# The decode's logits by one VectorE instruction each, in place of a product and a separate sum

## The chip, the cores and the metric

The program runs on one core of a Trainium2 chip. A core has a matrix engine (TensorE, PE in the profile), three engines for element-wise work (VectorE or DVE, ScalarE or ACT, GpSimd or POOL) and queues that start transfers (SP's and POOL's here). Each engine takes its instructions in order, and engines wait for each other by semaphores. The metric is device time in microseconds (us) for one execution of the whole program, the median of several.

## What is computed

One inference step of one layer of a hybrid decoder, for a prompt of 512 rows (with 16 learned rows ahead of it) and for 8 sequences that decode 4 rows each. All is fp32.

```python
h = rmsnorm(x, g_pre)
q, k, v, ga, cb, cc, ch, gc, ma, mc = jnp.split(h @ w_in, split_offsets(), axis=-1)
a = attend(q, k, v, b_sb).reshape(bsz, t, D_ATTN) * jax.nn.silu(ga)
u = cc * ch
u_ext = jnp.concatenate([conv_hist.astype(u.dtype), u], axis=1)
c = cb * causal_conv(u_ext, w_conv, b_conv) * jax.nn.silu(gc)
merged = (jax.nn.sigmoid(ma + b_gate[:D_MODEL]) * (a @ w_pa)
          + jax.nn.sigmoid(mc + b_gate[D_MODEL:]) * (c @ w_pc))
y = x + rmsnorm(merged @ w_out, g_post)
```

The width is 2048, and `w_in` has 12288 columns. Attention has 8 heads of 128 channels. It is a stick-breaking attention: from logits `z` come weights `sigmoid(z_ts) * prod(1 - sigmoid(z_tj))` over the later keys j, so all logits of a row must be there before its weights. The decode part reads a past of 512 keys for each of its 8 sequences, in 4 pages of 128 rows, found through a page table. Its logits are

```python
z = jnp.einsum('bqhd,bkhd->bhqk', q, k) * (HEAD_DIM ** -0.5) + b_sb[None, :, None, None]
```

that is, for every sequence, page, head and query row, 128 dot products of 128 channels: 8 x 4 x 8 x 4 = 1024 columns of 128 values.

## The kernel before

The kernel is written for a framework that takes a program in order, tracks which tile every instruction reads and writes, sets all semaphores, and orders each engine's instructions by a planner: among the instructions that a timing model says are ready, the one that stands first in the program goes first. `tc.keep_in_program_order` (also bound to the name `pin`) ties instructions together in the order in which they were written.

**TensorE's work.** Most products are made at fp32 accuracy out of three products of split numbers. `w_split` (L233) takes a block of 1024 x 128 weights, rounds it into `whi` on ScalarE (L236) and puts the rest into `wlo` on VectorE (L237). Both tiles have three buffers (pool `whl`). The matmuls of a block follow (L252 in the heads, L887 in the gates), 24 for each range of columns. `seven` (L890) makes a 2 x 2 block product out of seven products instead of eight; for that it forms sums of weight blocks on VectorE (L899, L902, L910, L915), and differences of results (L913, L918). The sums of the activations that it needs (tiles `t_hi`, `t_lo`) are made once, at L853 to L870, ahead of the gates.

**The stages.** After the norm and the first query projections come the attention heads 0 to 3 (`head_now`, L628) and the projections of heads 4 to 7 (`head_later`, L644). Then come the gates of the attention, the convolution (`conv_pair`, L952) and the gates of the merge (loop at L1029 and after), and then the remaining heads, the projections `w_pc`, `w_pa` and `w_out`, and the last norm.

**The decode's logits.** They run beside these stages, as a generator `decode_steps` (L669), of which `dec_step` takes one step at a time at fixed points of the program. There are 16 units (a half of the heads, a sequence) of 4 pages, 64 steps in all. The first 6 units (24 pages, `DEC1`) lie among the heads: `dec_step(64, "part")` at L833 sees that they are done in the program before the activations' sums. The other 10 units (40 pages) lie among the gates: `dec_group` (L813) takes two pages and one page by turns for the first 4 groups, one for the next 16, and again two and one by turns up to group 31. The two parts have pools of their own (`dec1`), whose room is given to later tiles. After them come the weights of the attention and the products with the values.

A step works like this. The query rows of the unit were loaded as two tiles `qt` (`qb` in the profile) of 2 query rows x 4 heads x 128 channels, copied to all 128 partitions. A page's keys `kt` (`kpage`), 128 rows x 512 channels for 4 heads, are loaded over POOL's queue; there are three such buffers. For each of the two query tiles, VectorE makes one product `pr` of 128 x 1024 values (L689). The sums over each 128 channels then go to `z_all`: ScalarE makes them one by one, as a copy into a tile `junk` with an accumulated sum (L695), or VectorE makes 4 or 8 of them at once (L698). The split by hand is: all 8 sums of the first tile on ScalarE; of the second, all 8 on VectorE, but in the second part 4 on ScalarE in each odd page.

## Time and profile before

| | us |
|---|---|
| runs of before | 1638.24, 1635.78, 1639.5 |
| median | 1638.24 |
| the profiled execution | 1638.43 |
| its span, first to last instruction | 1636.8 |
| TensorE (PE) busy | 1596.0 |
| VectorE (DVE) busy | 1259.1 |
| ScalarE (ACT) busy | 969.5 |

The profile names an instruction by its line in the kernel (L689), its engine, its operation and its tiles, output first. "Busy" counts an engine's instructions together without counting overlaps twice. A waiting row reads: engine and line, what released it, then the microseconds in total, the number of times and the longest. A window row has the stretch, its length, busy time and number of instructions for each engine, the clock granted to TensorE (1.00 is full speed), the share of DMA time and GB/s. In a row of a group of instructions stand the number of them, busy time, the mean duration of one in ns, and the engine's idle time before them.

### The profile page before, as it was taken

Reading aid. Unit: us, or ns where it says so; the run is one execution under the profiler, and the core shown is the slowest. Engines: PE = TensorE matmul, PEld = TensorE weight load, DVE = VectorE, ACT = ScalarE, POOL = GpSimd, SP = SyncE. Lnnn points to the kernel's source line nnn. Section 1 sums busy time; section 2 is a strip of 40 time slices with the busy share of each in tenths; the row PEclk is TensorE's granted clock in tenths of the full one; section 3 lists DMA queues with packets and bytes.
Section 4 is the critical chain, followed back from the end, with each engine's and each line's share of the span. In section 5 each row is a group of like instructions: output and inputs, shape, how many; then the busy total and the mean of one; then the engine's idle time right before and its main releaser. Section 6 shows DMA issues by size and latency. Waiting matters only on the chain.

```text
span 1636.8 us, 31603 instructions
## 1 busy us (share of the span) xinstructions
PE 1596.0 (98%) x12172; PEld 1534.2 (94%) x12172; DVE 1259.1 (77%) x1730; ACT 969.5 (59%) x2528; POOL 232.2 (14%) x418
## 2 busy tenths in 40 slices
PE   7999999999999999999999999999999999999997
PEld 6999999999999999999999999989877799999997
DVE  4537887797988988888988888876565567887776
ACT  6237887755775656565676667686544453355562
POOL 0033233322101000100011011002122110000000
PEclk7999999999999999999999999999999999999999
DMA  9254554545554444343555554446888545533345
GB/s 228 77 171 143 157 163 138 152 121 171 157 155 136 130 130 130 116 141 114 148 150 151 156 175 147 128 130 202 263 265 246 179 141 165 183 89 101 106 124 192
DMA packets 306813, 252.72 MB, mean 154 GB/s; under 512 B 11522, under 2 KB 276806, under 8 KB 305846
## 3 DMA queue, kind: packets, MB, share of 16 engines
q1 hardware_dynamic: 278165, 160.45, 34.3%
q0 software_dynamic: 28368, 89.98, 16.9%
q8 instruction: 95, 1.56, 0.4%
q14 instruction: 57, 0.46, 0.1%
q10 hardware_dynamic: 128, 0.27, 0.1%
HBM read 217.95 MB, written 32.71 MB: 153 GB/s over the span
## 4 chain that ended last, share of the span: by engine, by line
PE 75%; ACT 6%; DMA 5%; DVE 4%; issue 3%; POOL 0%; DVEq 0%; SPq 0%; POOLq 0%; ACTq 0%
PE mm L887 24%; PE mm L252 24%; PE o L887 20%; ACT junk L695 3%; PE tp L784 2%; ACT whi L236 2%; PE z L614 1%; DMA raw<-in_w_in 1%; PE o L624 1%; DVE pr L689 1%; DMA gt<-gate_scr 1%; DVE wlo L237 1%; PE z L545 1%; PE z L1319 1%; DMA kpage<-in_cache_k 1%
## 5 line engine op out<-in xcount | busy, mean ns | idle before, releaser
L236 ACT CAST whi<-raw 128x1024 fp32r<-128x1024 f32 x247 | 258.9, 1049 | 253.6 <-PE o L887 75.6
L237 DVE TENSOR_TENSOR wlo<-raw,whi 128x1024 fp32r<-128x1024 f32 x247 | 301.5, 1221 | 56.7 <-ACT whi L236 45.4
L887 PE MATMUL mm<-h_hi,whi 128*128 128x272 f32 (+1 forms) x1152 | 333.8, 290 | 2.8 <-ACT whi L236 2.8
L887 PE MATMUL mm<-h_lo,whi 128*128 128x272 f32 (+1 forms) x1152 | 332.4, 289 | 0.0
L887 PE MATMUL mm<-h_hi,wlo 128*128 128x272 f32 (+1 forms) x1152 | 331.6, 290 | 0.0
L887 PE MATMUL o<-t_hi,whi 128*128 128x272 f32 (+1 forms) x864 | 253.1, 293 | 8.7 <-ACT o L901 5.0
L887 PE MATMUL o<-t_hi,wlo 128*128 128x272 f32 (+1 forms) x864 | 250.8, 290 | 1.3 <-DVE wlo L237 1.3
L887 PE MATMUL o<-t_lo,whi 128*128 128x272 f32 (+1 forms) x864 | 250.6, 290 | 0.0
L237 DVE TENSOR_TENSOR wlo<-s,whi 128x1024 fp32r<-128x1024 f32 x126 | 154.2, 1224 | 100.5 <-ACT whi L236 100.2
L887 PEld LDWEIGHTS mm<-h_hi,whi 128*128 128x128 f32 x1152 | 217.7, 189 | 5.4 <-ACT whi L236 3.7
L887 PEld LDWEIGHTS mm<-h_hi,wlo 128*128 128x128 f32 x1152 | 216.6, 189 | 0.6 <-DVE dr L412 0.4
L887 PEld LDWEIGHTS mm<-h_lo,whi 128*128 128x128 f32 x1152 | 217.1, 188 | 0.1
L695 ACT ACTIVATE junk<-pr 128x128 f32<-128x128 f32 x592 | 182.6, 309 | 28.5 <-DVE pr L689 16.3
L236 ACT CAST whi<-s 128x1024 fp32r<-128x1024 f32 x126 | 131.5, 1044 | 96.9 <-PE o L887 30.8
L252 PE MATMUL mm<-h_hi,whi 128*128 128x280 f32 (+1 forms) x640 | 188.1, 294 | 0.0
L252 PE MATMUL mm<-h_hi,wlo 128*128 128x280 f32 (+1 forms) x640 | 188.0, 295 | 0.0
L252 PE MATMUL mm<-h_lo,whi 128*128 128x280 f32 (+1 forms) x640 | 187.6, 293 | 0.0
L887 PEld LDWEIGHTS o<-t_hi,whi 128*128 128x128 f32 x864 | 163.6, 189 | 15.5 <-ACT o L901 6.1
L887 PEld LDWEIGHTS o<-t_hi,wlo 128*128 128x128 f32 x864 | 163.8, 190 | 2.2 <-DVE wlo L237 2.2
L887 PEld LDWEIGHTS o<-t_lo,whi 128*128 128x128 f32 x864 | 164.4, 190 | 0.0
L689 DVE TENSOR_TENSOR pr<-kpage,qb 128x1024 f32<-128x1024 f32 x128 | 152.3, 1218 | 10.7 <-DMA qb<-q_scr 6.5
L252 PEld LDWEIGHTS mm<-h_hi,whi 128*128 128x128 f32 x640 | 121.4, 190 | 0.7
(392 smaller groups left out, 3402.3 us busy)
## 6 DMA issues: line engine op xcount, KB each, us to landing
raw<-in_w_in SPq DMA_DIRECT2D x192, 512.0 KB, 4.3
kpage<-in_cache_k POOLq DMA_DIRECT2D x64, 256.0 KB, 3.4
qb<-q_scr POOLq DMA_DIRECT2D x32, 512.0 KB, 5.7
vpage<-in_cache_v POOLq DMA_DIRECT2D x64, 256.0 KB, 6.1
raw<-in_w_out SPq DMA_DIRECT2D x32, 512.0 KB, 4.0
gate_scr<-g POOLq DMA_DIRECT2D x32, 272.0 KB, 3.5
gt<-gate_scr POOLq DMA_DIRECT2D x16, 544.0 KB, 4.2
raw<-in_w_pc SPq DMA_DIRECT2D x16, 512.0 KB, 5.9
```

What stands on the lines that cost most here:

```text
L236: act.copy(hi, x)
L237: dve.tensor_sub(lo, x, hi.bitcast(F32))
L252: pe.matmul(o, lhsT=w, rhs=r[:, t0:t1], start=(k == 0 and n == 0), stop=(k == nk - 1 and n == 2))
L545: pe.matmul(zt[:m, c0:c0 + n], lhsT=l[:, s0:s0 + m], rhs=r[:, ts:ts + n], start=(c0 == 0 and i == 0), stop=(i == 2), skip_group_check=True)
L614: pe.matmul(o, lhsT=l, rhs=x, start=False, stop=(i == len(ops) - 1), skip_group_check=True)
L624: pe.matmul(ot[:, ts - NMETA:ts - NMETA + n], lhsT=l[:m, st, :], rhs=x[:m, c0:c0 + n], start=False, stop=(g == GROUPS[-1] and i == 2), ski ...
L689: dve.tensor_mul(pr, kt.unsqueeze(1).broadcast_to([P, 2, 512]), qt))
L695: act.activation(junk, pr[:, t, h * P:(h + 1) * P], AF.Copy, accum_out=z_all[:, pg, b, 4 * hf + h, 2 * i + t:2 * i + t + 1])
L784: pe.matmul(po[32 * j:32 * (j + 1), :], lhsT=lhs, rhs=rhs, start=(pg == 0), stop=(pg == NPG), tile_position=(0, 32 * j), skip_group_check= ...
L887: pe.matmul(o, lhsT=l[:, k, :], rhs=r, start=(start and k == 0 and m == 0), stop=(stop and k == 7 and m == 2), skip_group_check=True)
L1319: pin(pe.matmul(o, lhsT=(m1, m2)[h][:, k + 8 * (q == 1), ts], rhs=two[h][q == 2][:, :, k, :], start=(n == 0), stop=(n == 47)))
```

## The change

The product, the sums on ScalarE and the sums on VectorE go, and with them the tile `pr`. In their place VectorE runs one instruction for each query row and head, which multiplies 128 x 128 keys by the query and sums the products along the channels into one column of `z_all`. Its product goes to a tile `junk` of 128 x 128, now with two buffers. The instructions are not held in program order.

```diff
                         for i, qt in enumerate(qts):
-                            pr = d1.tile([P, 2, 512], F32, name="pr", bufs=2)
-                            tc.keep_in_program_order(
-                                dve.tensor_mul(pr, kt.unsqueeze(1).broadcast_to([P, 2, 512]), qt))
-                            n = 2 if i == 0 else int(said == "logits" and pg % 2)
-                            if n:
-                                for t in range(n):
-                                    for h in range(4):
-                                        junk = d1.tile([P, P], F32, name="junk", bufs=1)
-                                        act.activation(junk, pr[:, t, h * P:(h + 1) * P], AF.Copy,
-                                                       accum_out=z_all[:, pg, b, 4 * hf + h, 2 * i + t:2 * i + t + 1])
-                            if n < 2:
-                                dve.reduce_sum(
-                                    z_all[:, pg, b, 4 * hf:4 * hf + 4, 2 + n:4].rearrange("p h t -> p t h"),
-                                    pr[:, n:].rearrange("p t (h d) -> p t h d", d=P), axis=mybir.AxisListType.X)
+                            for t in range(2):
+                                for h in range(4):
+                                    junk = d1.tile([P, P], F32, name="junk", bufs=2)
+                                    dve.tensor_tensor_reduce(
+                                        out=junk, in0=kt[:, h * P:(h + 1) * P], in1=qt[:, t, h * P:(h + 1) * P],
+                                        scale=1.0, scalar=0.0, op0=ALU.mult, op1=ALU.add,
+                                        accum_out=z_all[:, pg, b, 4 * hf + h, 2 * i + t:2 * i + t + 1])
                         yield
```

## The prediction

> **What bounds the kernel now.** I read the page first: the span, the busy shares, and the chain that ended last.

> ```profile
> span 1636.8 us, 31603 instructions
> PE 1596.0 (98%) x12172; PEld 1534.2 (94%) x12172; DVE 1259.1 (77%) x1730; ACT 969.5 (59%) x2528; POOL 232.2 (14%) x418
> ...
> DVE  4537887797988988888988888876565567887776
> ...
> PE 75%; ACT 6%; DMA 5%; DVE 4%; issue 3%; POOL 0%; DVEq 0%; SPq 0%; POOLq 0%; ACTq 0%
> ```

> TensorE (PE) sets the time: it is busy for 98% of the span and carries 75% of the chain. An average hides the stages, though, and VectorE (DVE) stands at 8 or 9 tenths in most slices of the first two thirds. That is where the decode's logits run, by the first and last start in this row of the tile `junk`:

> ```profile
> L695 ACT ACTIVATION_READ_ACCUMULATOR junk<-pr x592: 185/187/203, 116.8 to 1077.6; 128x1 f32 x198
> ```

> So I cut that stretch into stages and read the windows: stage A (the attention heads), a change-over, stage B (gates and convolution), stage C (gates with more decode pages). The columns are window, PE, PEld, DVE, ACT and POOL busy, clock, DMA share, GB/s. The second fence is the same windows for DVE's instructions on the tile `pr` alone, that is the products and the sums on DVE.

> ```profile
> 115.00:345.00 230.00, 227.77 (x1730) 222.13 (x1729) 188.15 (x258) 174.67 (x597) 72.59 (x130) 0.99 0.51 153
> 345.00:415.00 70.00, 68.65 (x541) 67.84 (x540) 58.62 (x78) 38.88 (x80) 16.80 (x28) 1.00 0.49 152
> 415.00:820.00 405.00, 402.83 (x3177) 401.28 (x3176) 359.93 (x428) 247.63 (x674) 34.72 (x61) 1.00 0.46 136
> 820.00:1080.00 260.00, 254.43 (x1986) 252.16 (x1985) 217.77 (x214) 183.21 (x536) 25.10 (x44) 0.99 0.51 150
> sum 965.00, PE 953.69 PEld 943.41 DVE 824.48 ACT 644.38 POOL 149.22; mean PE 238.42 PEld 235.85 DVE 206.12 ACT 161.10 POOL 37.30
> ```

> ```profile
> 115.00:345.00 230.00, 86.88 (x72) 0.99 0.51 153
> 345.00:415.00 70.00, 4.80 (x4) 1.00 0.49 152
> 415.00:820.00 405.00, 67.98 (x62) 1.00 0.46 136
> 820.00:1080.00 260.00, 59.70 (x54) 0.99 0.51 150
> sum 965.00, DVE 219.36; mean DVE 54.84
> ```

> Three things are to be seen. PE idles 965 − 953.69 = 11.3 us in the whole stretch, which is all that any relief there could win. DVE has 965 − 824.48 = 140.5 us left, 42, 11, 45 and 42 us by stage. ScalarE (ACT) has 320 us left, so it is DVE that must not get more work here. What PE waits for in this stretch:

> ```profile
> PE o L887 <- DVE c L913: 3.5, 4, 1.9
> PE tp L445 <- ACT nat L443: 2.2, 1, 2.2
> PE mm L887 <- ACT whi L236: 2.2, 3, 0.7
> PE o L887 <- ACT o L901: 1.9, 4, 1.4
> PE o L887 <- DVE wlo L237: 1.3, 4, 0.3
> PE o L887 <- ACT s L908: 0.2, 1, 0.2
> ```

> ACT is named for 2.2 + 2.2 + 1.9 + 0.2 = 6.5 us, DVE for 4.8 us.

> **What the change removes.** It takes off DVE the 219.4 us of the fence above (128 products and 64 sums), and off ACT these two rows:

> ```profile
> L695 ACT ACTIVATE junk<-pr 128x128 f32<-128x128 f32 x592 | 182.6, 309 | 28.5 <-DVE pr L689 16.3
> ...
> L695 ACT ACTIVATION_READ_ACCUMULATOR junk<-pr 128x1 f32 x592 | 110.8, 187 | 0.0
> ```

> On ACT that is at most 293 us. Since PE waits only 6.5 us for ACT, the relief is worth 6.5 us at the very most, and I count it as nothing: PE and DVE hide it.

> **What it adds.** Per page, 2 query tiles × 2 rows × 4 heads = 16 instructions on DVE; 64 pages make 1024. The trace of before has no such instruction, so its price is bounded by neighbours. On DVE an instruction's duration overlaps the next one's, so I take start to start:

> ```profile
> 440.31 1.22 DVE L910 TENSOR_TENSOR raw<-raw 128x1024 f32<-128x1024 f32 x1
> 441.45 0.43 DVE L913 TENSOR_TENSOR c<-o,s 128x272 f32<-128x272 f32 x1
> 441.81 1.23 DVE L237 TENSOR_TENSOR wlo<-raw,whi 128x1024 fp32r<-128x1024 f32 x1
> ```

> 1024 elements take 1.14 us and 272 take 0.36 us: 0.78/752 = 1.04 ns an element. So 128 elements take 0.36 − 144 × 1.04 ns = 0.21 us. That is the lower end: the sum comes free. How a sum leaves an engine is seen on ACT:

> ```profile
> 166.31 0.31 ACT L695 ACTIVATE junk<-pr 128x128 f32<-128x128 f32 x1 [0.96 <-DVE pr L689]
> 166.52 0.19 ACT L695 ACTIVATION_READ_ACCUMULATOR junk<-pr 128x1 f32 x1
> 166.74 0.31 ACT L695 ACTIVATE junk<-pr 128x128 f32<-128x128 f32 x1
> ```

> A second instruction reads the accumulator, 0.22 us start to start behind 0.21 us of main work. If DVE's read cost as much as ACT's, a sum would take 0.43 us. But DVE's own tiny instructions are cheaper:

> ```profile
> 592.30 0.16 DVE L970 TENSOR_TENSOR u<-c,cv 128x2 f32<-128x2 f32 x1
> 592.38 0.40 DVE L971 TENSOR_TENSOR u<-c,cv 128x240 f32<-128x240 f32 x1
> ```

> Two elements take 0.08 us. A read on DVE is nearer to this row than to ACT's, so I take 0.21 + 0.09 = **0.30 us** a sum, 4.8 us a page, and keep 0.21 and 0.43 as ends. The highest thinkable value, half rate with the dear read, adds another 128 × 1.04 ns = 0.13 us: 0.56 us.

> [...]

> So DVE loses 219.4 us and gains 1024 × 0.30 = 307.2 us, net +87.8 us. The total would still fit in 140.5 us of idle time, but not all idle time can be filled, because weight splits arrive in bursts. These windows show how full DVE gets now:

> ```profile
> 600.00:640.00 40.00, 39.66 (x316) 39.41 (x315) 37.67 (x46) 24.44 (x66) 4.54 (x8) 1.00 0.50 146
> 680.00:720.00 40.00, 39.67 (x316) 39.39 (x315) 37.37 (x50) 24.86 (x70) 4.65 (x8) 1.00 0.45 133
> 760.00:800.00 40.00, 39.67 (x314) 39.39 (x314) 38.86 (x55) 24.68 (x69) 4.63 (x8) 1.00 0.41 121
> ```

> At 37.4 to 38.9 of 40 us PE begins to lose (0.33 us each). I take the lowest, 37.37/40 = 0.93, as the share that DVE can hold over a stage, and 0.97 as the upper end. A stage then lasts the longer of its present time and DVE's work divided by 0.93. The pages per stage are the products of the `pr` rows by two: 24, 1.5, 20.5, 18.

> - A: 188.15 − 86.88 + 24 × 4.8 = 216.5; /0.93 = 232.8, against 230: +2.8 us.
> - Change-over: 58.62 − 4.80 + 1.5 × 4.8 = 61.0; /0.93 = 65.6, under 70: nothing; DVE's and PE's own work hide it. That cover is thin: if A's pages run late, the sums for the next stage start late.
> - B: 359.93 − 67.98 + 20.5 × 4.8 = 390.4; /0.93 = 419.7, against 405: +14.7 us.
> - C: 217.77 − 59.70 + 18 × 4.8 = 244.5; /0.93 = 262.9, against 260: +2.9 us.

> Together +20.4 us. The thin cover is this row:

> ```profile
> 333.60 0.73 DVE L859 TENSOR_TENSOR r<-h_hi 128x548 f32<-128x548 f32 x1 [0.51 <-ACT junk L695]
> ```

> The block sums of the gate stage start only when the first decode part has freed its room, and ACT's last sum frees it now. That wait of 0.51 us goes; what is late next is DVE's own last sum.

> **Waits and queues.** The edit drops the pinned order of the product and the exchange of `pr` between DVE and ACT; no wait is added, but 16 instructions of one page stand in DVE's in-order queue without a gap: 4.8 us, two pages 9.6 us. Behind them stand the weight splits (L237), and PE waits for those. A split buffer holds three half-blocks, so PE can live on some of them; I put this into the 0.93. On POOL a page's load waits until DVE is done with an earlier page:

> ```profile
> POOL kpage L667 <- DVE pr L689: 305.3, 45, 17.0
> ```

> POOL's other stores queue behind that wait. It is as long as DVE is late, and the same loads are issued, no DMA more. I price it at nothing since POOL is at 14%; without that cover a late load would show as DVE waiting for `kpage`.

> **Rivals.** *Dear sum.* DVE's read costs as ACT's, 0.43 us, 6.88 us a page. By the same steps A is 101.27 + 165.1 = 266.4 (/0.93 = 286.4, +56), change-over 64.1 (/0.93 = 69, nothing), B 433.0 (465.6, +61), C 281.9 (303.1, +43): +160 us, 1798 us. With the cheap read and half rate it is 0.21 + 0.13 + 0.08 = 0.42 us and about the same; with both, 0.56 us, A +110, change-over +2, B +106, C +83: +301 us, 1940 us. For it: ACT's row. Against half rate:

> ```profile
> 9.24 1.28 DVE L205 SCALAR_TENSOR_TENSOR hn<-xt,rs,g_bc 128x1024 f32<-128x1024 f32 x1
> ```

> This two-source fp32 form takes 1.28 us for 1024 elements, where half rate would need 2 × 1024 × 1.04 ns = 2.13 us. [...]

> *It fits.* The planner orders the small, unpinned instructions into the gaps, DVE holds 0.97: A 223, B 402.4, C 252, none longer than now. Time unchanged, 1638 us. For it: 140.5 us of idle time against 87.8 us. Against it: the three full windows, where PE loses already.

> *Faster.* The sum comes free at 0.21 us, 3.36 us a page. DVE's work falls to 181.9, 360.8 and 218.6 us, level or below today's, and PE gets back what it waits for ACT, up to 6.5 us: 1632 us. This decides below about 0.214 us a sum, where 1024 × it equals 219.4 us. Against it: ACT's second instruction.

> *The change doesn't do what it says.* Were the instruction built out of two full passes on DVE, the sum would be 0.42 us, priced above.

> **How the numbers follow.** The profiled execution took 1638.43 us with a span of 1636.8; the median of the runs shown is 1638.24, so I add to 1638.4. Forecast (0.26 to 0.36 us a sum, some tens of us): 1638.4 + 20.4 = **1658.8 us**, chance 0.47. Dear sum 0.25, it fits 0.16, faster 0.12. The range runs from 1632 (the whole relief of ACT) up to 1790, just short of the dear-read sum; beyond it remain the dearest cases. Of "it fits" a little ends outside the bound of 0.2%, about what a measurement of this kernel can tell from no change: faster 0.12, same 0.15, slower 0.73.

> **What would show it.** 1024 instructions on L689's place, each with a read beside it; start to start 0.30 us (0.21 or 0.43 would speak for a rival). DVE near 1347 us of busy time, ACT near 680 to 730. PE's waits for `wlo`, under 2 us in the stretch now, grow to tens of us, most in stage B. A wrong price moves the time by about 1 us per ns once DVE is full; a better order than 0.93 would make the time stay.

## The result and the profile after

The kernel became faster, where slower was forecast.

| | before | after |
|---|---|---|
| median of the runs, us | 1637.23 (1635.78 to 1639.5, 4 runs) | 1621.05 (1620.66 to 1621.63, 4 runs) |
| ratio after/before | | 0.9895, 95% interval 0.9877 to 0.9913 |
| the profiled execution, us (its span) | 1638.43 (1636.8) | 1621.34 (1619.7) |
| forecast, us (range) | | 1658.8 (1632 to 1790) |

The page of after: the span, busy time, VectorE's row of the 40 slices, the chain of waits, and the group of the new instruction (count | busy, mean ns | idle time before them).

```profile
span 1619.7 us, 32340 instructions
PE 1589.6 (98%) x12172; PEld 1531.2 (95%) x12172; DVE 1267.9 (78%) x3586; ACT 755.7 (47%) x1339; POOL 241.0 (15%) x418
...
DVE  4529999666999999999999976676555568887776
...
PE 85%; DMA 4%; issue 2%; DVE 1%; ACT 1%; POOL 1%; DVEq 0%; POOLq 0%; ACTq 0%; SPq 0%
...
L690 DVE CUSTOM_DVE_ANT_0 junk<-kpage,qb 128x128 f32<-128x128 f32 x1024 | 244.7, 286 | 10.6 <-DMA qb<-q_scr 7.0
```

VectorE's busy time rose by 8.8 us and not by the 87.8 forecast, and ScalarE's fell by 213.8. VectorE stands at 9 tenths or more over most of the logits' stretch, fuller than before, and yet TensorE's share of the chain rose from 75% to 85%. The price of a sum stands in the timeline of after (start, duration, instruction):

The read of the accumulator is there, 0.08 to 0.09 us long, but the next instruction starts at the same instant as the read. From sum to sum it is 0.21 us. All 1024 come to 1024 x 0.21 = 215 us, level with the 219.4 us removed.

Where the time came from is seen in the stages A, change-over, B and C in the windows of after, and in one more window behind them, of before (first row) and of after (second):

```profile
115.00:345.00 230.00, 227.21 (x1725) 221.31 (x1724) 205.91 (x986) 114.23 (x223) 79.91 (x130) 0.99 0.50 154
345.00:415.00 70.00, 69.52 (x547) 68.65 (x546) 37.38 (x68) 29.47 (x50) 16.35 (x27) 1.00 0.48 146
415.00:820.00 405.00, 404.88 (x3203) 404.44 (x3202) 390.60 (x1297) 175.29 (x265) 42.28 (x73) 1.00 0.50 148
820.00:1080.00 260.00, 260.00 (x2062) 259.39 (x2061) 211.80 (x499) 129.69 (x183) 21.78 (x37) 1.00 0.47 143
```

```profile
1080.00:1180.00 100.00, 96.26 (x707) 86.49 (x706) 62.93 (x73) 62.50 (x87) 21.08 (x36) 1.00 0.66 204
```

```profile
1080.00:1180.00 100.00, 100.00 (x744) 91.10 (x743) 62.60 (x81) 54.88 (x79) 20.32 (x36) 1.00 0.73 227
```

Read the matmul counts, not the busy time. Over B and C TensorE's busy time grew by only 404.88 + 260.00 − 402.83 − 254.43 = 7.6 us, but it started 3203 + 2062 − 3177 − 1986 = 102 matmuls more. In a row they start every 0.125 to 0.126 us, so it was 12.9 us further on at 1080. Behind that, from 1080 to 1180 us, 3.7 us of idle time went, most of it one wait of 3.1 us for ScalarE's `o`; why it goes was not taken apart. Together that is 16.6 of the 17.1 us by which the profiled times differ; A and the change-over, with one matmul more between them, give nothing.

Why is the progress, 12.9 us, larger than the fall of the idle time, 7.6? One place in before shows both reasons. Its timeline on VectorE, on TensorE, and its windows (the clock is the third number from the end):

```profile
851.08 2.35 DVE L689 TENSOR_TENSOR pr<-kpage,qb 128x1024 f32<-128x1024 f32 x2
853.34 1.22 DVE L910 TENSOR_TENSOR raw<-raw 128x1024 f32<-128x1024 f32 x1
854.48 0.44 DVE L913 TENSOR_TENSOR c<-o,s 128x272 f32<-128x272 f32 x1
```

```profile
852.75 0.29 PE L887 MATMUL mm<-h_lo,whi 128*128 128x272 f32 x1
854.97 0.39 PE L887 MATMUL o<-t_hi,whi 128*128 128x272 f32 x1 [1.93 <-DVE c L913]
```

```profile
853.00:855.00 2.00, 0.07 (x2) 0.03 (x1) 2.00 (x4) 1.91 (x9) 0.54 (x1) 1.00 0.68 193
855.00:858.00 3.00, 3.00 (x14) 3.00 (x15) 3.00 (x3) 1.88 (x8) 0.00 (x0) 0.54 0.26 85
```

Two decode products stand in VectorE's queue ahead of the difference `c` that frees TensorE's result. TensorE waits 1.93 us, and then runs 3 us at a clock of 0.54, with 14 matmuls where 24 would fit (3/0.125). That costs another 1.2 us, which no idle time shows. This is the smaller reason: it is the only such stretch of before in B and C.

The larger one is how idle time is counted. A matmul is recorded with 0.29 us, but the next can start 0.126 us after it, so the idle time leaves out about 0.16 us of every gap. Here the starts are 852.75 and 854.97: 2.22 us in place of 0.126, so 2.09 us are lost where the wait says 1.93. Outside the slow stretch, B and C of before have 43 gaps of more than 0.2 us from start to start. They lose 12.9 us, of which the idle time shows 7.7; in after it is 16 gaps and 1.7 us, of which it shows 0.1. That leaves 3.6 us unseen, and the slow stretch 1.5, of the 5.3 us between progress and idle time.

### The profile page after: what moved, and what is told of

It reads as the page before. It is cut to its first block, busy times and chain, and to the rows that moved or that the text cites. A ratio compares the mean times of both kernels' runs of the same rounds, so it can differ in the third digit from the quotient of the medians.

```text
span 1619.7 us, 32340 instructions
## 1 busy us (share of the span) xinstructions
PE 1589.6 (98%) x12172; PEld 1531.2 (95%) x12172; DVE 1267.9 (78%) x3586; ACT 755.7 (47%) x1339; POOL 241.0 (15%) x418
## 4 chain that ended last, share of the span: by engine, by line
PE 85%; DMA 4%; issue 2%; DVE 1%; ACT 1%; POOL 1%; DVEq 0%; POOLq 0%; ACTq 0%; SPq 0%
PE mm L880 31%; PE o L880 23%; PE mm L252 22%; PE tp L777 2%; PE z L614 1%; PE o L624 1%; DMA gt<-gate_scr 1%; PE z L545 1%; PE z L1312 1%; DMA kpage<-in_cache_k 1%; DMA cr<-c_scr 0%; PE z L1166 0%; DMA gate_scr<-gt 0%; PE tp L442 0%; DMA out<-nat 0%
## 5 line engine op out<-in xcount | busy, mean ns | idle before, releaser
L236 ACT CAST whi<-raw 128x1024 fp32r<-128x1024 f32 x247 | 259.6, 1051 | 327.8 <-PE mm L880 112.5
L237 DVE TENSOR_TENSOR wlo<-raw,whi 128x1024 fp32r<-128x1024 f32 x247 | 301.8, 1222 | 72.4 <-ACT whi L236 60.9
L690 DVE CUSTOM_DVE_ANT_0 junk<-kpage,qb 128x128 f32<-128x128 f32 x1024 | 244.7, 286 | 10.6 <-DMA qb<-q_scr 7.0
L880 PEld LDWEIGHTS mm<-h_lo,whi 128*128 128x128 f32 x1152 | 216.8, 188 | 0.0
L237 DVE TENSOR_TENSOR wlo<-s,whi 128x1024 fp32r<-128x1024 f32 x126 | 154.7, 1228 | 69.5 <-ACT whi L236 68.3
L236 ACT CAST whi<-s 128x1024 fp32r<-128x1024 f32 x126 | 132.0, 1048 | 158.9 <-PE mm L880 50.1
L252 PEld LDWEIGHTS mm<-h_lo,whi 128*128 128x128 f32 x640 | 121.0, 189 | 0.6
```

The costliest lines, as they stand in the source:

```text
L236: act.copy(hi, x)
L237: dve.tensor_sub(lo, x, hi.bitcast(F32))
L252: pe.matmul(o, lhsT=w, rhs=r[:, t0:t1], start=(k == 0 and n == 0), stop=(k == nk - 1 and n == 2))
L690: dve.tensor_tensor_reduce(out=junk, in0=kt[:, h * P:(h + 1) * P], in1=qt[:, t, h * P:(h + 1) * P], scale=1.0, scalar=0.0, op0=ALU.mult, o ...
L880: pe.matmul(o, lhsT=l[:, k, :], rhs=r, start=(start and k == 0 and m == 0), stop=(stop and k == 7 and m == 2), skip_group_check=True)
```

## The experiments

E1 to E8 ask for the relief of ScalarE, the order, and VectorE's load; the others, but for E11, for the size and the rows of the decode's work in VectorE's queue. Each ratio is to the kernel before. "Pinned" is held in program order. "Last sum" is the start of the last logit instruction.

### E1: after, with every sum pinned

```diff
-                                    dve.tensor_tensor_reduce(
+                                    pin(dve.tensor_tensor_reduce(
```

> The changed kernel with each of its 1024 sums held behind the VectorE instruction written before it, so that a page's sums can no longer run ahead of their place in the program. Work on every engine is as in the changed kernel (1621 us). Theory order (the gain comes from the freedom of the sums to fill VectorE's gaps ahead of their place): most of the gain goes, 1631 to 1640 us, and the last sum starts near 1040 to 1080 us instead of 933. Theory relief (the gain comes from the 237 us taken off ScalarE): stays within 1618 to 1625 us.

1622.56 us, ratio 0.9913 (0.9893 to 0.9933). The free sums of after ran ahead (last one at 933 us); pinned, the last starts at 1060, not far from before (last product at 1071, last sum at 1078), and the gain stays. The dropped pin is not its cause.

### E2: before, with the product unpinned

```diff
-                            tc.keep_in_program_order(
-                                dve.tensor_mul(pr, kt.unsqueeze(1).broadcast_to([P, 2, 512]), qt))
+                            dve.tensor_mul(pr, kt.unsqueeze(1).broadcast_to([P, 2, 512]), qt)
```

> The kernel before (1637 us) with the product no longer held in program order; ScalarE keeps its 592 sums. Theory order: 1619 to 1628 us, the last product well before 1000 us. Theory relief: 1634 to 1640 us.

1674.35 us, 1.0232 (1.021 to 1.0255). The products ran ahead (last at 714 us) and ScalarE's sums with them (last at 722), ahead of the roundings `whi` in its queue. TensorE's waits, 115 to 1080 us:

```profile
PE o L886 <- ACT whi L236: 14.1, 10, 2.6
PE mm L886 <- ACT whi L236: 6.5, 12, 1.3
```

The same freedom that costs nothing with the new sums costs 37 us with products and sums on two engines.

### E3: after, with 592 sums on ScalarE over the keys

```diff
+                            n = 2 if i == 0 else int(said == "logits" and pg % 2)
+                            for t in range(n):
+                                for h in range(4):
+                                    aj = d1.tile([P, P], F32, name="aj", bufs=1)
+                                    az = d1.tile([P, 1], F32, name="az", bufs=2)
+                                    act.activation(aj, kt[:, h * P:(h + 1) * P], AF.Copy, accum_out=az)
```

> The changed kernel with 592 sums of 128 channels put back on ScalarE as extra work (over the keys alone, results unused), so ScalarE's load is about that of before. Theory relief: 1632 to 1640 us, with PE waiting for ScalarE again. Theory order: within 1619 to 1626 us.

1648.0 us, 1.0066 (1.0047 to 1.0086). This looked like proof that ScalarE's load costs 27 us, but the page of this kernel names another reason:

```profile
L699 ACT ACTIVATE aj<-kpage 128x128 f32<-128x128 f32 x592 | 182.8, 309 | 79.4 <-DMA kpage<-in_cache_k 68.2
```

ScalarE's in-order queue stood still for 68.2 us at these sums, waiting for transfers of keys. So the run adds a wait and not only load; E11 adds load alone.

### E4: after, with 8 more sums a page

```diff
+                                    if i == 1:
+                                        more = d1.tile([P, 1], F32, name="more", bufs=2)
+                                        dve.tensor_tensor_reduce(
+                                            out=junk, in0=kt[:, h * P:(h + 1) * P], in1=qt[:, t, h * P:(h + 1) * P],
+                                            scale=1.0, scalar=0.0, op0=ALU.mult, op1=ALU.add, accum_out=more)
```

> The changed kernel with the 8 sums of the second query tile made twice in each page: 512 more, about 0.21 us each, 108 us more on VectorE, results unused. This is about the load that the prediction gave VectorE with its price of 0.30 us (88 us more). By the prediction's step (VectorE holds 0.93 of a stage) VectorE's 830 us between 115 and 1062 become 938, which need 1009 us: 1675 to 1690 us. At 0.97: about 1642 us. If gaps can be filled to the end: 1621 to 1630 us.

1653.36 us, 1.0095 (1.0075 to 1.0115), with VectorE's busy time at 1374.1, above the 1347 that the forecast foresaw. It is close to the forecast's time, but not by its reason: the stages B and C lose nothing. The time goes at the change-over (first matmul of the gates' products with `t_hi` at 399.5 us in place of 388.5) and behind the logits, whose last sum now starts at 1152, so that the later products of the decode follow late (the last matmul on `c_hl` ends at 1362.7 in place of 1327.7).

### E5: E1 with 592 sums on ScalarE over what VectorE's sums leave

```diff
-                                    junk = d1.tile([P, P], F32, name="junk", bufs=2)
+                                    junk = d1.tile([P, P], F32, name="junk", bufs=16)
...
+                                    if t < (2 if i == 0 else int(said == "logits" and pg % 2)):
+                                        aj = d1.tile([P, P], F32, name="aj", bufs=1)
+                                        az = d1.tile([P, 1], F32, name="az", bufs=2)
+                                        act.activation(aj, junk, AF.Copy, accum_out=az)
```

> The changed kernel with its sums held in program order (1622.6 us) and, as extra work, ScalarE's 592 sums where the kernel before has them, each over the product tile that a held VectorE instruction left (results unused). Unlike the free sums of the run before this one with ScalarE's load (1648 us), these can't bunch ahead. Theory relief (ScalarE's queue is what PE waited for): 1634 to 1641 us. Theory granularity (PE waited because VectorE worked in pieces of 1.1 to 2.3 us, and ScalarE's load only hurts when it bunches): 1620 to 1626 us.

1664.33 us, 1.0164 (1.0133 to 1.0195). It looked as if the hand-over from VectorE to ScalarE cost 42 us. The edit has a second part, though, 16 result tiles in place of 2; E13 and E14 take the two apart.

### E6: before without ScalarE's sums

```diff
-                            if n:
-                                for t in range(n):
-                                    for h in range(4):
-                                        junk = d1.tile([P, P], F32, name="junk", bufs=1)
-                                        act.activation(junk, pr[:, t, h * P:(h + 1) * P], AF.Copy,
-                                                       accum_out=z_all[:, pg, b, 4 * hf + h, 2 * i + t:2 * i + t + 1])
```

> The kernel before with ScalarE's 592 sums left out (those logits keep zeros); VectorE's products and sums as before. Theory relief: 1619 to 1625 us, the whole gain without any change on VectorE. Theory granularity: 1632 to 1638 us.

The kernel leaves these logits out (they keep zeros, written once by GpSimd). 1632.71 us, 0.9968 (0.9955 to 0.9981): the whole relief of ScalarE alone is worth some 5 us (1637.23 x 0.0032), within the 6.5 that the prediction gave as its most. TensorE still waits 4.3 us for `c`, behind the products.

### E7: before with all sums on VectorE

```diff
-                            n = 2 if i == 0 else int(said == "logits" and pg % 2)
+                            n = 0
...
-                                    z_all[:, pg, b, 4 * hf:4 * hf + 4, 2 + n:4].rearrange("p h t -> p t h"),
+                                    z_all[:, pg, b, 4 * hf:4 * hf + 4, 2 * i:2 * i + 2].rearrange("p h t -> p t h"),
```

> The kernel before with all sums made by VectorE's reduction, 8 at once: ScalarE is relieved of all 592, VectorE gets 84 half-size reductions more or about 71 us (128 reductions of 1.13 us instead of 44 of 1.13 and 20 of 0.59). It tells what the relief is worth when it is paid with a dearer sum. By the run with 108 us more on VectorE (+32 us over 1621) 71 us cost about 21 us: 1640 to 1646 us. If VectorE's gaps take them for nothing: 1620 to 1626 us.

1683.65 us, 1.0275 (1.0244 to 1.0305), at a VectorE busy time of 1332.4, less than E4's 1374.1. It is slower by 46 us where E6, which only drops these sums, is faster by 5: moving them to VectorE does not win by itself, and the form in which VectorE takes them matters. 19.0 us of it are one wait of TensorE at the change-over.

### E8: E1 with 8 more pinned sums a page

The edit is that of E4, with the added sums pinned.

> The changed kernel held in program order (1622.6 us) with the 8 sums of the second query tile made twice, held too: 108 us more on VectorE, which can't be put off. If the 32 us of the free version came from VectorE being full (PE waits for the weight splits): 1650 to 1660 us again or more. If they came from the logits ending late, at 1152 us, and pushing the decode's tail behind: 1630 to 1645 us, with the last sum near 1070 to 1090 us.

1664.49 us, 1.016 (1.013 to 1.0189). TensorE's waits, the start of the block sums of the activations (L859 before, shifted to L857 here), and the windows of B and C:

```profile
PE mm L885 <- ACT whi L236: 20.3, 1, 20.3
```

```profile
L857 DVE TENSOR_TENSOR r<-h_hi x4: 721/722/729, 367.9 to 369.8; 128x548 f32<-128x548 f32 x4
```

```profile
415.00:820.00 405.00, 405.00 (x3206) 404.79 (x3206) 385.41 (x1229) 178.16 (x271) 31.13 (x56) 1.00 0.44 131
820.00:1080.00 260.00, 260.00 (x2067) 260.00 (x2066) 245.48 (x852) 122.61 (x170) 27.09 (x47) 1.00 0.52 159
```

One wait of 20.3 us at the change-over; B and C run as in after, with VectorE at 95 and 94%. The rest is lost behind the logits, whose last sum starts at 1200 us.

### E9 and E10: E1 in one or two larger pieces a query tile

These leave the logits out (the sums don't follow the heads), and keep VectorE's time: one sum over 1536 products in place of eight over 128 (E9), or two over 768 (E10).

```diff
+                            junk = d1.tile([P, 3, 512], F32, name="junk", bufs=1)
+                            pin(dve.tensor_tensor_reduce(
+                                out=junk, in0=kt.unsqueeze(1).broadcast_to([P, 3, 512]),
+                                in1=qt[:, 0, :].unsqueeze(1).broadcast_to([P, 3, 512]),
...
+                                junk = d1.tile([P, 2, 384], F32, name="junk", bufs=2)
+                                pin(dve.tensor_tensor_reduce(
+                                    out=junk, in0=kt[:, 0:384].unsqueeze(1).broadcast_to([P, 2, 384]),
+                                    in1=qt[:, :, 0:384],
```

> The changed kernel held in program order (1622.6 us), but for each query tile one instruction over 3 x 512 channels in place of 8 over 128: VectorE's time for a page stays (2 x 1.67 us against 16 x 0.21 us), in pieces of 1.67 us. It leaves the logits out (the columns get other sums or zeros). ScalarE has no sums, as in the changed kernel. Theory granularity (short urgent instructions of VectorE stand behind long pieces in its queue): 1630 to 1636 us, as the kernel before without ScalarE's sums (1632.7). Theory totals (only the engines' loads count): 1620 to 1625 us.

> As the run before it, in two instructions over 768 channels for each query tile, pieces of 0.87 us (4 a page, 3.5 us). It leaves the logits out too. Granularity: between, 1625 to 1631 us. Totals: 1620 to 1625 us.

E9 1636.2 us, 0.9991 (0.9976 to 1.0005); E10 1650.03, 1.0074 (1.0049 to 1.0099), with VectorE busy for 1263.2 and 1273.6 us. The gain of the change is gone, at nearly the same load and without any sum on ScalarE. But the smaller pieces lose more, which "the size of a piece" does not explain. In the written order of VectorE's instructions, E9's pieces stand alone 116 times out of 128 (it has one result tile); E10's stand in twos 77 times out of 157 rows (it has two). This gave the next theory: the length of the row.

### E11: E1 with 592 sums on ScalarE over constants

```diff
+                                        pin(act.activation(aj, ident, AF.Copy, accum_out=az))
```

> The changed kernel held in program order with 592 sums on ScalarE over a constant tile, held at the places of the sums before, so that they wait neither for VectorE nor for a transfer. If ScalarE's load alone delays PE: 1640 to 1665 us, as with the sums over VectorE's products (1664). If those 42 us came from ScalarE waiting in its queue for VectorE's products: 1623 to 1630 us.

1620.67 us, 0.9896 (0.9871 to 0.9922), with ScalarE busy for 965.9 us, as much as before. ScalarE's load as such costs nothing that the time shows (E1, without it, has 1622.56).

### E12 and E13: E1 with 8 and with 16 result tiles

Nothing but the number of result tiles changes. How many sums the planner writes in a row depends on it: with 2 tiles mostly two, with 16 mostly 8 to 16.

```diff
-                                    junk = d1.tile([P, P], F32, name="junk", bufs=2)
+                                    junk = d1.tile([P, P], F32, name="junk", bufs=16)
```

> The kernel after with every sum held in program order, as in the first experiment, and with 8 result tiles (junk) instead of 2. Nothing else differs: the same 1024 sums, the same work on ScalarE. What changes is how many sums stand in a row in VectorE's queue: in the written order of the first experiment 324 rows, most of them of 2 sums (0.42 us); here 190 rows, many of 5 to 8 (1.05 to 1.7 us). Theory 'length of the row' (what costs is how long the decode's work stands in one piece ahead of a weight split or a gate's operation): between the fine pieces (1622.6) and the one-piece form (1636.2), 1626 to 1640 us, with PE waits for wlo, whi or c back. Rival 'form of the piece' (the one-piece kernel lost by its own form, its wide result or its waits for pages, not by the row): 1622 us as in the first experiment, within 3 us.

> The same with 16 result tiles: 67 rows, most of 8 to 16 sums (1.7 to 3.4 us), and no sums on ScalarE. It is also the fifth experiment (1664.3 us, 106 rows) without ScalarE's sums over the products. Theory 'length of the row': slower than with 8 results, 1635 to 1665 us; if it comes near 1664, the row explains the fifth experiment too, and the hand-over to ScalarE was worth little. Rival 'hand-over' (the fifth experiment lost because ScalarE stood waiting for VectorE's products): 1622 to 1630 us here.

E12 1648.27 us, 1.0072 (1.0058 to 1.0085), beyond the end of what was expected; E13 1662.13, 1.0156 (1.0143 to 1.017). VectorE is busy for 1265.4 and 1268.8 us, as in after. That is 40 us for the order of the same instructions. In E13's trace, the first and the last of the 18 sums of one row and what stands behind them, then TensorE's timeline at that place, then its waits from 115 to 1080 us:

```profile
1028.97 0.28 DVE L690 CUSTOM_DVE_ANT_0 junk<-kpage,qb 128x128 f32<-128x128 f32 x1
...
1032.58 0.28 DVE L690 CUSTOM_DVE_ANT_0 junk<-kpage,qb 128x128 f32<-128x128 f32 x1
1032.80 0.08 DVE L690 DVE_READ_ACCUMULATOR2_ANT z_all<- 128x1 f32 x1
1032.80 0.43 DVE L911 TENSOR_TENSOR c<-mm,s 128x272 f32<-128x272 f32 x1
...
1033.57 1.22 DVE L237 TENSOR_TENSOR wlo<-raw,whi 128x1024 fp32r<-128x1024 f32 x1
```

```profile
1032.56 0.29 PE L880 MATMUL mm<-h_lo,whi 128*128 128x272 f32 x1
1034.84 0.39 PE L880 MATMUL mm<-h_hi,wlo 128*128 128x272 f32 x1 [2.00 <-DVE wlo L237]
```

```profile
PE o L880 <- DVE wlo L237: 11.8, 5, 6.0
PE mm L880 <- DVE wlo L237: 8.8, 5, 2.0
PE mm L880 <- ACT whi L236: 6.4, 9, 0.8
```

The row keeps VectorE from 1028.97 to 1032.80. The split `wlo` stands behind it and TensorE waits 2.00 us. What TensorE waits for in this kernel is, for the most part, the split. The longest wait, 6.0 us, has the same form at the change-over: a row of 32 sums, 405.64 to 412.45 us, and the split behind it. In E12 it is mostly the difference `c` that comes late (10.6 us in 13 waits).

### E14: E5 with 4 result tiles in place of 16

```diff
-                                    junk = d1.tile([P, P], F32, name="junk", bufs=16)
+                                    junk = d1.tile([P, P], F32, name="junk", bufs=4)
```

> The fifth experiment (592 sums of ScalarE over the products that VectorE's sums leave, 1664.3 us) with 4 result tiles instead of 16: the rows of VectorE's sums become short (332 rows, most of 1 to 4), but ScalarE still stands behind VectorE's products, and now VectorE behind ScalarE's reads of the 4 tiles. Theory 'length of the row': near the first experiment, 1620 to 1635 us, although ScalarE's busy time stays near 970. Rival 'hand-over': as slow as the fifth experiment or slower, 1655 to 1680 us, as the two engines wait for each other more often.

1623.22 us, 0.9919 (0.9906 to 0.9933): ScalarE is busy for 959.7 us, with 592 sums behind VectorE's products, and it is as fast as E1. With E13 (E5 without ScalarE's sums, 1662.1 against 1664.3) it settles E5: the rows were the cost, the hand-over cost next to nothing.

### E15: before in pieces of half the size

```diff
-                            pr = d1.tile([P, 2, 512], F32, name="pr", bufs=2)
-                            tc.keep_in_program_order(
-                                dve.tensor_mul(pr, kt.unsqueeze(1).broadcast_to([P, 2, 512]), qt))
+                            for t in range(2):
+                                pr = d1.tile([P, 512], F32, name="pr", bufs=2)
+                                tc.keep_in_program_order(dve.tensor_mul(pr, kt, qt[:, t]))
```

The sums follow for one query row at a time, on ScalarE where they were there before.

> The kernel before with pieces of half the size: one product tile of 128x512 per query row (two buffers as before), so 256 products of about 0.61 us in place of 128 of 1.14 us, and VectorE's sums 4 at a time; ScalarE keeps its 592 sums. VectorE gets some 10 to 15 us more work. In the written order the products stand 125 times alone, 56 times in twos (1.2 us) and 5 times in more; in the kernel before 34 alone and 47 in twos (2.3 us). Theory 'length of the row': faster than before in spite of more work on VectorE, 1622 to 1632 us, and fewer PE waits behind L913 and wlo. Rival 'what the rows of 16 sums show has no part in the kernel before': no gain, 1636 to 1650 us for the added work.

1629.85 us, 0.9957 (0.9944 to 0.9971), with 16.1 us more busy time on VectorE (1275.2) and ScalarE's 592 sums in place. So the kernel before lost by its rows too: shorter ones win 7 us without the new instruction. The windows of change-over, B and C say more:

```profile
345.00:415.00 70.00, 63.35 (x461) 62.06 (x460) 54.93 (x78) 34.55 (x70) 16.05 (x27) 0.93 0.43 135
415.00:820.00 405.00, 405.00 (x3207) 404.78 (x3206) 365.79 (x479) 244.26 (x670) 34.28 (x60) 1.00 0.46 135
820.00:1080.00 260.00, 260.00 (x2064) 259.81 (x2064) 231.63 (x272) 192.51 (x562) 26.90 (x47) 1.00 0.52 160
```

In B and C TensorE shows no idle time, and starts as many matmuls as in after, although VectorE is busier than in before and ScalarE keeps its sums. So the loss there goes with the size of the pieces, and neither with VectorE's load nor with ScalarE's. What keeps E15 8.8 us behind after comes for the most part at the change-over, with 86 matmuls fewer than in after. TensorE waits 4.6 us there for a difference `c`, and VectorE, which has to make it, had stood idle for 7.2 us until a transfer of weights (`raw`) landed. Why that transfer is late in this kernel stays open.

### E16: after with one result tile

```diff
-                                    junk = d1.tile([P, P], F32, name="junk", bufs=2)
+                                    junk = d1.tile([P, P], F32, name="junk", bufs=1)
```

> The kernel after with one result tile (junk) instead of two: in the written order 520 rows of sums, 343 of them of a single one, in place of 359 rows, most of them of two. Theory 'length of the row': 0.21 us more or less in a row is below what TensorE's buffers carry, since hardly any wait is left in that stretch: 1619 to 1623 us, the same as after; slower only if the one tile makes the sums wait for each other (VectorE's start to start above 0.21 us).

1641.08 us, 1.0025 (1.0012 to 1.0037): not the same as after, but the case that was named as the exception. Two successive sums, the start of the block sums, TensorE's longest wait, and TensorE's windows behind it:

```profile
333.25 0.29 DVE L690 CUSTOM_DVE_ANT_0 junk<-kpage,qb 128x128 f32<-128x128 f32 x1
333.58 0.29 DVE L690 CUSTOM_DVE_ANT_0 junk<-kpage,qb 128x128 f32<-128x128 f32 x1
```

```profile
L852 DVE TENSOR_TENSOR r<-h_hi x4: 721/722/730, 349.6 to 351.5; 128x548 f32<-128x548 f32 x4
```

```profile
PE mm L880 <- ACT whi L236: 9.0, 1, 9.0
```

```profile
389.00:393.00 4.00, 0.00 (x0) 0.00 (x0) 3.86 (x5) 1.34 (x2) 1.01 (x2) 0.50 0.00 0
393.00:397.00 4.00, 3.15 (x12) 2.83 (x13) 2.83 (x3) 1.45 (x3) 2.81 (x5) 0.50 0.88 218
397.00:401.00 4.00, 3.26 (x18) 3.04 (x16) 1.00 (x5) 2.17 (x3) 0.00 (x0) 0.71 0.98 350
```

Two sums in a row start 0.33 us apart here, which comes near the price that the prediction took. VectorE is busy for 1317.4 us, 49.5 more than in after, and the time is 20 us above after's, about the term forecast for 87.8 us more. It is not lost in B, where the forecast put 14.7: TensorE loses 0.7 us between 415 and 1080 us, by the measure of the table below. About half of it is lost at the change-over (9.0 us and a clock of 0.50 to 0.71 behind it) and the rest behind the logits, whose last sum starts at 1108 us in place of 933.

## The rows and the time, together

A row is a run of decode instructions on VectorE with nothing else between them. Mean lengths are worked out from the traces, for rows that start between 415 and 1080 us. Beside them stands what TensorE's matmuls lost in that window: the sum of all start-to-start gaps above 0.2 us, less 0.126 for each. The times are medians; the profiled executions of E9 and E10 took 1630.7 and 1644.8 us, some 5 us less, so their medians may have lost more than the table shows.

| kernel | mean row, us | matmuls lost, us | time, us |
|---|---|---|---|
| E16 one tile | 0.51 | 0.7 | 1641.1 |
| after | 0.62 | 1.7 | 1621.1 |
| E8 pinned, 8 more sums | 0.63 | 0.7 | 1664.5 |
| E4 8 more sums | 0.64 | 1.0 | 1653.4 |
| E1 pinned | 0.65 | 4.6 | 1622.6 |
| E11 with ScalarE load | 0.66 | 2.3 | 1620.7 |
| E14 four tiles, sums on ScalarE | 0.69 | 3.7 | 1623.2 |
| E15 before, half pieces | 0.96 | 0.9 | 1629.9 |
| E12 eight tiles | 1.18 | 23.5 | 1648.3 |
| E10 two pieces | 1.50 | 19.9 | 1650.0 |
| before | 1.64 | 14.3 | 1637.2 |
| E6 before, no sums on ScalarE | 1.65 | 13.1 | 1632.7 |
| E7 before, all sums on VectorE | 1.69 | 29.8 | 1683.7 |
| E9 one piece | 1.75 | 8.8 | 1636.2 |
| E5 sixteen tiles, sums on ScalarE | 2.32 | 32.6 | 1664.3 |
| E13 sixteen tiles | 2.75 | 34.5 | 1662.1 |

Up to a mean row of 1 us the matmuls lose next to nothing in this window; above, 9 to 35 us. E4, E8 and E16 are slow all the same, since they lose their time outside it. Among the long rows the length doesn't order the kernels: E9 and before lose less than E12 with shorter rows. Where in the sequence of splits and differences a row falls probably counts too; that was not tried. E2 (52.2 us at 1.48) and E3 (22.0 at 0.62) stand outside the table, since ScalarE's own queue is late in them.

## Why the prediction was wrong

**The step that failed** is the one under "Waits and queues": 16 instructions of a page were to stand in VectorE's queue without a gap, 4.8 us, and to be covered by the share of 0.93. It had the sign of the edit wrong. With two result tiles the planner writes the sums mostly in twos, 0.42 us, between the splits; it was the kernel before that had the long row, two products in 2.35 us. In the windows of 600 to 800 us, in which TensorE lost 0.33 us each, its one wait is for a split `wlo` that stands behind two products and 1.4 us of the convolution's work; it did not lose by VectorE being 93% full. From 600 to 640 us E15 has VectorE busy for 39.08 of 40 us with TensorE busy for all 40. And after holds in B's 405 us the 390.60 us of VectorE's work, 96%, that the forecast's share stretched to 419.7, with TensorE idle for 0.12 us.

**The price of a sum** was the term of the greatest effect: 0.30 us taken, 0.21 measured. The main instruction was sized right; the read was put at 0.09 us on top, and its duration was right too (0.08 to 0.09), but the next instruction starts at the same instant as the read. This alone takes +87.8 us down to nothing, and the +20.4 us with it. As on ScalarE, a sum on VectorE is two instructions, the main one and a read: the trace of after has 1024 of each, and the read adds nothing from sum to sum. No run shows the half rate that the prediction adds in its dearest cases, 0.13 us a sum and so a part of the 0.42 us, the 0.56 us and the 1940 us: it was the author's assumption. What the runs showed in its place is E9's row:

```profile
L689 DVE CUSTOM_DVE_ANT_1 junk<-kpage,qb 128x1536 f32<-128x1536 f32 x128 | 224.2, 1751 | 5.2 <-DMA qb<-q_scr 3.8
```

1536 elements in 1.75 us are 1.14 ns each, not 2 x 1.04, and after's sums of 128 elements start 0.21 us apart, the price without half rate.

**The relief of ScalarE** "at most 6.5 us": right (E6, 5 us; E11, none). But the prediction made it the floor of the whole range. The rival *faster* had the price right and took only this as its gain, 1632 us. TensorE's waits for VectorE, 4.8 us, were read as the mark of a full engine that can only get worse; they were the cheapest thing to win, and they understated it. "All that any relief there could win", 11.3 us of idle time, was too low for the same reason: by the counts of matmuls 12.9 us were won in B and C alone, where the idle time fell by 7.6.

**The thin cover** at the change-over was named and then costed at nothing. There a third to a half of what added load costs does arise. The start of the block sums and TensorE's wait for `whi` ahead of the first products with them, by kernel: E1 320.1, before 333.6 and E15 334.5 us, no such wait; E4 348.0, 4.2 us; E16 349.6, 9.0; E7 364.8, 19.0; E8 367.9, 20.3. The cover ends between 335 and 348 us. After has it at 285.2.

**The fill terms** +14.7 for B and +2.9 for C: refuted by E4, E8 and E16, in which B and C lost nothing.

**The marks** named in "What would show it": start to start 0.21 us spoke for the rival; VectorE near 1347 us did not come (1267.9); ScalarE near 680 to 730 came out higher (755.7), as the two rows taken off, 293 us, overlap in time; 213.8 were freed; waits for `wlo` of tens of us in B did not come (0.5 us in after, from 115 to 1080 us), but did, 11.8 + 8.8 us, when E13 made the rows that the prediction feared.

## What to carry to other kernels

Work of low urgency on an in-order engine can cost more by the length of its uninterrupted row ahead of urgent work than by its total: here the same 1024 instructions gave 1622 or 1662 us, and the number of result buffers set the row. The total isn't free either: with rows as short, added load cost 20 to 43 us (E16, E4, E8 against after), not spread over the stages but at the change-over and behind the logits. So ask of an added instruction first how many of it will stand together, and what the critical engine has in hand meanwhile. Breaking up instructions helped here even on a VectorE that was nearly full: E15, with its products halved, took 1629.85 us in place of 1637.23, with the 39.08 of 40 us above. And count the bound engine's instructions in a window beside its busy time: recorded durations that overlap (0.29 us, at starts 0.126 us apart) hid about 0.16 us of each gap here, and the clock of 0.54 behind the stall in before shows as no idle time at all.

## What the runs showed of the hardware

In after an accumulator read on VectorE cost no time of its own where other work followed it: sum to sum 0.21 us, and a read of 0.08 to 0.09 us starts at the same instant as the next instruction. With one result tile (E16) it was 0.33 us from sum to sum, and whether that is the tile's release or the read's end was not taken apart.

Behind a wait of TensorE of 1.93 us the granted clock was 0.54 over the next 3 us (before, at 853 us), and behind one of 9.0 us it was 0.50 and 0.71 over the next eight (E16). Not each such wait had it: behind E13's 2.00 us at 1033 the matmuls soon started 0.12 to 0.13 us apart again. What decides it was not shown.

```profile
1035.07 0.29 PE L880 MATMUL mm<-h_hi,whi 128*128 128x272 f32 x1
1035.19 0.29 PE L880 MATMUL mm<-h_lo,whi 128*128 128x272 f32 x1
1035.32 0.29 PE L880 MATMUL mm<-h_hi,wlo 128*128 128x272 f32 x1
```

And 210 us more busy time on ScalarE cost nothing (E11 1620.67 us, E1 1622.56), though TensorE needs its roundings. They came early enough even in E14, where that queue stood 27.0 us in all for VectorE's sums and no wait of TensorE for `whi` shows from 60 to 1110 us, but not in E3, where it stood 68.2 us for transfers and TensorE waited 6.8 us for `whi` (115 to 1080 us).
